# A fourth output weight split later, a fourth tile's sum begun earlier, and a last quarter taken by feature block, in the output projection of a decoder's second layer

## The chip, the core and the metric

The kernel runs on one core of a Trainium2 chip. The core has a matrix engine (TensorE, PE in the profile, with PEld for its weight loads), a vector engine (VectorE, DVE), a scalar engine (ScalarE, ACT), a general engine (GpSimd, POOL) and a queue engine (SyncE, SP), which here only starts transfers from the chip's memory. Each engine runs its own instructions in order; across engines they wait for each other by semaphores. The metric is the time of one execution on the device in microseconds, lower is better.

## What is computed

Two decoder layers on 512 tokens of 1024 features in float32. Layer A is a latent attention, layer B a sliding-window attention with 16 query heads of 64 features on 4 shared key and value heads. After each attention stands an output projection, a residual sum with layer norm, and a squared-ReLU MLP with its own norm. The change touches layer B's attention and output projection:

```python
def _swa(x, w_q, sinks, w_o, k_band, v_band, rel_bias):
    q = (x @ w_q).reshape(B, nb, BLOCK, SWA_KV_HEADS, G, SWA_HEAD_DIM)
    s = jnp.einsum('bnqkgd,bnjkd->bnkgqj', q, k_band).astype(jnp.float32) * SWA_HEAD_DIM ** -0.5
    ...
    p = (p / denom[..., None]).astype(x.dtype)
    o = jnp.einsum('bnkgqj,bnjkd->bnqkgd', p, v_band).reshape(B, S, SWA_Q_HEADS * SWA_HEAD_DIM)
    return o @ w_o

        ...
        x = _layernorm(alpha * x + y, ln_mix_g[l], ln_mix_b[l])
        x = _layernorm(alpha * x + _mlp(x, mlp_w_up[l], mlp_w_down[l]), ln_mlp_g[l], ln_mlp_b[l])
```

## The kernel before

**Splits.** Every float32 operand of a large product is split into a high and a low half (`split`, lines 75 to 84): ScalarE rounds the value into the high half (line 77), then VectorE, or GpSimd for some, subtracts that from the value for the low half (line 81). A product takes three matmuls per block of 128 features: high by high, high by low, low by high (`three`). Weights go through a stream (`queue`, `weights`, `prepare`): a weight tile of 128 by 1024 is loaded by SyncE into one of two `raw` buffers, and split into one of four pairs `wh` and `wl`. A raw buffer is free for the next load when the split has read it, a pair when the last matmul has read it. `fetchers` start a load ahead of its split, and `state["hold"]` says how far the stream may be prepared.

**Layer B's attention** is a hand-written software pipeline (`run_steps`): at step u it issues head u+2's scores and softmax, then some filling work, then head u's transposes (`turn`), and at each odd step the output of a pair of heads (`mix`). `mix` for heads 2m and 2m+1 leaves feature block m of the attention's output: TensorE multiplies probabilities and values, ScalarE copies half of each of two results (`low`, one buffer), VectorE adds (`o`), then ScalarE and GpSimd split `o` into `oh` and `ol`. Blocks 0 to 3 lie in the first tile of `oh` and `ol`, blocks 4 to 7 in the second. GpSimd also scales each head's probabilities (`p`, line 1449) and masks its transposed ones (`pm`, line 1469).

**The output projection** (`TokMajor`, object `proj`) has four token tiles t and two halves of the output's columns. Weight kp of a half covers feature blocks 2kp and 2kp+1. In the first half each token tile has a sum in PSUM, to which `part(t, kp)` adds six matmuls; after kp = 3 the sum is added to the residual on VectorE (line 638) and counted for the norm (line 631). The filling list places parts amid the attention:

```python
            for t, kp, u in ((0, 0, 11), (0, 1, 12), (1, 0, 12), (1, 1, 13), (2, 0, 14), (2, 1, 14), (0, 2, 15), (1, 2, 16), (2, 2, 16)):
                if (t, kp) == (1, 1):
                    fill.append((0, 13, 13, last_loads))
```

What the list leaves over, tile 3 and all of kp = 3, is done by `finish` after the last `mix`, weight by weight and tile by tile. Then `finish` takes the second half of the columns: four more weights, 24 matmuls for each token tile, each tile followed by its norm. `last_loads` prepares the fourth weight (load and split), fetches the seventh and eighth into a spare buffer, and lets the stream run on. The fourth weight's split is issued behind a softmax exponential (`"exp" if c == 3`).

The order of TensorE and of some transfers is the program's; the order on the other engines is made by a scheduler when the program is built, under the data's dependencies and the `behind` rules. While the second half runs, ScalarE and VectorE also split the MLP's first weights, into tiles `w_fac` and `w_quada`, whose room is the attention's.

Of the kernel before, what the change touches and what calls it, by code (L numbers as in the profile page):

```python
# [48 lines left out]
def build(tc, nc, io, out):  # L49
    with ExitStack() as top:  # L50
# [24 lines left out]
        def split(dst_h, dst_l, src, engine=None, keep=False):  # L75

            high = nc.scalar.activation(dst_h, src, AF.Copy)  # L77
            if keep:
                pe(high)
            with behind(state.pop("open", None)):  # L80
                low = (engine or nc.vector).tensor_sub(dst_l, src, f32(dst_h))  # L81
            if pinned[0] and engine is None:
                pe(low)
            return high, low
# [18 lines left out]
        def group(dst, pairs, first=True, last=True, **kw):  # L103
            for i, (st, mv) in enumerate(pairs):
                pe(nc.tensor.matmul(  # L105
                    dst, st, mv, start=first and i == 0, stop=last and i == len(pairs) - 1, **kw
                ))
# [207 lines left out]
            queue("w_sq", io["w_sq"][m], nc.gpsimd if m > 1 else nc.vector)  # L315
        first_so = len(stream)
        for c in range(8):
            queue("w_so", io["w_so"][c], nc.gpsimd if c in POOL_SO else nc.vector, "exp" if c == 3 else None)
        mlp_stream(1)

        ready = {}
# [199 lines left out]
        class TokMajor:  # L521
# [5 lines left out]
                self.src, self.evac, self.name = src, evac, name  # L527
                self.w, self.b, self.done = [], {}, set()

            def group(self, b, t, kp, w, cols=slice(0, 512)):  # L530
                tk = slice(t * P, (t + 1) * P)
                wh, wl = w
                for kk in range(2):
                    k, c = 2 * kp + kk, slice(kk * 512 + cols.start, kk * 512 + cols.stop)
                    group(b, three(self.src.h(k, tk), self.src.l(k, tk), wh[:, c], wl[:, c]), k == 0, k == 7)

            def part(self, t, kp):
# [4 lines left out]
                self.group(self.b[t], t, kp, self.w[kp])  # L542
                self.done.add((t, kp))
                if kp == 3:
                    self.evac(t, slice(0, 512), self.b[t])

            def finish(self, gb=None, dst=None, early=None, gb_at=None):

                for kp in range(4):
                    for t in range(NT):
                        if (t, kp) not in self.done:
                            self.part(t, kp)
                    if kp == gb_at:
                        gb = gb()
                if gb is not None:
                    ws = [weights(self.name) for _ in range(4)]
                    if callable(gb):
                        gb = gb()  # L560
                    for t in range(NT):
                        end = dst is None and t == NT - 1
                        n = 2 if end else 1
                        if end:
                            parts = last_tokens(gb)
                        for i in range(n):
                            c = slice(i * 512 // n, (i + 1) * 512 // n)
                            b = bank(512 // n)
                            for kp in range(4):
                                self.group(b, t, kp, ws[kp], c)  # L570
                            pinned[0] = early
                            with tc.high_priority():
                                self.evac(t, slice(512 + c.start, 512 + c.stop), b)
                            pinned[0] = False
                        pinned[0] = early
                        with tc.high_priority():
                            if end:
                                last_norm(gb, *parts)
                            else:
                                layer_norm(t, gb, dst)  # L580
                        if early:
                            prepare(early[t])
                        pinned[0] = False
                        if dst is not None and t in (1, 2):
                            with tc.high_priority():
# [730 lines left out]
        with tc.tile_pool(name="swa", bufs=1) as mp:  # L1316
# [120 lines left out]
            def weigh(h, bs, nb, sm, ri):  # L1437
                p = mp.tile([P, NT, P], F32, tag="p", bufs=3, name=nm("p"))
                for n in range(NT):
                    state["exp"] = nc.scalar.activation(  # L1440
                        p[:, n, :], bs[n // 2][:, n % 2, P:], AF.Exp, bias=nb[:, n : n + 1],
                        scale=SWA_SCALE, accum_out=sm[:, n : n + 1],
                    )
# [3 lines left out]
                nc.vector.reciprocal(ri, sm)  # L1447
                with tc.high_priority():
                    muls[h] = nc.gpsimd.tensor_mul(p, p, ri.unsqueeze(2).broadcast_to([P, NT, P]))
                ps_of[h] = p  # L1450
# [20 lines left out]
            def mix(h):  # L1471
# [7 lines left out]
                for n2 in range(2):  # L1479
# [18 lines left out]
                    for a, to in enumerate((lo, hi)):  # L1498
# [1 line left out]
                            o[to, n2, :].rearrange("p (n q) -> p n q", n=2),  # L1500
                            parts[lo, :, a, :], low[:, :, a, :],
                        )
                split(oh[m // 4][:, m % 4, :], ol[m // 4][:, m % 4, :], o.rearrange("p a b -> p (a b)"), nc.gpsimd)

            proj = TokMajor(Pair(oh, ol), add_scaled_last, "w_so")

            def last_loads():
                prepare(1)
                fetch_two(first_so + 6, xp.tile([P, 2, 1024], F32, tag="xt", bufs=8, name=nm("raw2")))
                state["hold"] = len(stream)  # L1510

            fill = []
# [136 lines left out]
```

## Time and profile before

| | |
|---|---|
| median of 3 runs | 993.61 us (993.2 to 993.73) |
| profiled execution | 994.75 us, its span 993.0 us |
| mean granted TensorE clock | 0.996 |
| TensorE busy, 493 to 620 us (layer B's keys to its attention's end) | 123.48 of 127.00 us |
| TensorE busy, 620 to 690 us (the output projection's rest and the MLP's start) | 68.56 of 70.00 us, clock 0.95 |

The span runs from the first to the last instruction of one profiled execution. Busy times of TensorE overlap with the next instruction's, since matmuls are pipelined: a matmul of 128 by 512 shows 0.39 us but starts 0.23 us after the one ahead. The granted clock is the share of full speed at which TensorE ran; that is why a row below 1 matters even where the engine shows no idle time. Names in the rows are the program's tiles without buffer numbers, and an idle time ahead of an instruction stands in brackets with the instruction that ended it.

### The profile page before, as it was taken

Reading aid. Unit: us, or ns where it says so; the run is one execution under the profiler, and the core shown is the slowest. Engines: PE = TensorE matmul, PEld = TensorE weight load, DVE = VectorE, ACT = ScalarE, POOL = GpSimd, SP = SyncE. Lnnn points to the kernel's source line nnn. Section 1 sums busy time; section 2 is a strip of 40 time slices with the busy share of each in tenths; the row PEclk is TensorE's granted clock in tenths of the full one; section 3 lists DMA queues with packets and bytes.
Section 4 is the critical chain, followed back from the end, with each engine's and each line's share of the span. In section 5 each row is a group of like instructions: output and inputs, shape, how many; then the busy total and the mean of one; then the engine's idle time right before and its main releaser. Section 6 shows DMA issues by size and latency. Waiting matters only on the chain.

```text
span 993.0 us, 15665 instructions
## 1 busy us (share of the span) xinstructions
PE 982.1 (99%) x6028; PEld 883.6 (89%) x6028; DVE 772.3 (78%) x1279; ACT 545.0 (55%) x842; POOL 239.0 (24%) x207
## 2 busy tenths in 40 slices
PE   9999999999999999999999998999999999999998
PEld 9888888998899999998898886889998999999986
DVE  6589858989768779786686787698885986898756
ACT  5557644467547537646146786436763663664620
POOL 1231101121312212210002997512131122022000
PEclk9999999999999999999999999899999999999999
DMA  7421236399888978964132223338896796898332
GB/s 262 145 88 43 93 120 201 54 230 220 146 198 227 168 169 224 224 106 147 65 107 96 86 92 132 106 65 147 268 183 121 233 214 116 223 261 147 84 127 85
DMA packets 60678, 149.54 MB, mean 151 GB/s; under 512 B 5259, under 2 KB 10300, under 8 KB 60604
## 3 DMA queue, kind: packets, MB, share of 16 engines
q0 software_dynamic: 24320, 58.73, 33.6%
q1 hardware_dynamic: 36140, 89.56, 26.2%
q8 instruction: 47, 0.77, 0.3%
q10 hardware_dynamic: 144, 0.26, 0.1%
q14 instruction: 27, 0.22, 0.1%
HBM read 146.41 MB, written 4.22 MB: 152 GB/s over the span
## 4 chain that ended last, share of the span: by engine, by line
PE 94%; DVE 2%; ACT 1%; POOL 1%; issue 0%; DMA 0%; DVEq 0%; POOLq 0%; ACTq 0%
PE mm L105 86%; PE tr L105 5%; PE tr L1243 1%; POOL wl L81 1%; PE tr L742 1%; ACT p L1440 1%; ACT wh L77 0%; PE tr L1465 0%; DMA raw<-in_w_h 0%; PE tr L507 0%; DVE o L1499 0%; POOL ol L81 0%; DVE pt L81 0%; DVE mm L1430 0%; PE tr L1007 0%
## 5 line engine op out<-in xcount | busy, mean ns | idle before, releaser
L105 PE MATMUL mm<-wh,fac 128*128 128x512 f32 (+1 forms) x944 | 292.7, 387 | 0.0
L77 ACT ACTIVATE wh<-wq 128x1024 fp32r<-128x1024 f32 x164 | 173.7, 1060 | 184.7 <-PE mm L105 138.4
L81 DVE TENSOR_TENSOR wl<-wq,wh 128x1024 fp32r<-128x1024 f32 x164 | 199.4, 1221 | 67.4 <-ACT wh L77 66.5
L105 PE MATMUL mm<-xth,wh 128*128 128x256 f32 (+1 forms) x928 | 243.8, 291 | 0.0
L105 PE MATMUL mm<-xth,wl 128*128 128x256 f32 (+1 forms) x800 | 233.8, 292 | 0.0
L105 PEld LDWEIGHTS mm<-wh,fac 128*128 128x128 f32 x944 | 176.4, 188 | 35.2 <-DVE fac L81 0.6
L105 PE MATMUL mm<-xtl,wh 128*128 128x256 f32 (+1 forms) x672 | 197.4, 294 | 0.0
L105 PE MATMUL mm<-wl,fac 128*128 128x512 f32 (+1 forms) x472 | 182.6, 387 | 0.0
L105 PEld LDWEIGHTS mm<-xth,wh 128*128 128x128 f32 x928 | 168.9, 192 | 3.0
L105 PEld LDWEIGHTS mm<-xth,wl 128*128 128x128 f32 x800 | 153.5, 192 | 2.7
L105 PEld LDWEIGHTS mm<-xtl,wh 128*128 128x128 f32 x672 | 128.9, 192 | 3.0
L77 ACT ACTIVATE wh<-raw 128x1024 fp32r<-128x1024 f32 (+3 forms) x86 | 85.0, 989 | 78.4 <-PE mm L105 53.2
L204 POOL DMA_DIRECT2D wq<-in_up x64 | 77.6, 1238 | 200.3 <-DVE wl L81 193.0
L105 PEld LDWEIGHTS mm<-wl,fac 128*128 128x128 f32 x472 | 88.9, 188 | 16.7
L81 DVE TENSOR_TENSOR wl<-raw,wh 128x1024 fp32r<-128x1024 f32 (+2 forms) x64 | 76.0, 1197 | 32.6 <-ACT wh L77 32.4
L204 POOL DMA_DIRECT2D wq<-in_down x48 | 42.0, 875 | 189.1 <-DVE wl L81 183.2
L81 POOL TENSOR_TENSOR wl<-raw,wh 128x1024 fp32r<-128x1024 f32 (+2 forms) x22 | 47.0, 2140 | 90.7 <-ACT wh L77 67.9
L105 PE MATMUL mm<-wh,oh 128*128 128x512 f32 x128 | 51.3, 400 | 3.2 <-ACT oh L77 3.2
L105 PE MATMUL mm<-wh,ol 128*128 128x512 f32 x128 | 50.8, 397 | 1.5 <-POOL ol L81 1.5
L105 PE MATMUL mm<-wl,oh 128*128 128x512 f32 x128 | 50.4, 394 | 0.1
L443 POOL TENSOR_TENSOR rs<-mv,half 128x1 f32<-128x1 f32 x16 | 8.8, 553 | 168.1 <-DVE mv L488 163.4
L641 DVE TENSOR_TENSOR x<-mm,x 128x512 f32<-128x512 f32 (+1 forms) x49 | 32.9, 675 | 15.6 <-PE mm L105 15.5
(246 smaller groups left out, 1791.1 us busy)
## 6 DMA issues: line engine op xcount, KB each, us to landing
wq<-in_up POOLq DMA_DIRECT2D x64, 512.0 KB, 7.3
wq<-in_down POOLq DMA_DIRECT2D x48, 512.0 KB, 7.1
wq<-in_up SPq DMA_DIRECT2D x32, 512.0 KB, 6.6
raw<-in_down SPq DMA_DIRECT2D x28, 512.0 KB, 6.1
wq<-in_down SPq DMA_DIRECT2D x24, 512.0 KB, 5.4
raw<-in_up SPq DMA_DIRECT2D x16, 512.0 KB, 4.7
raw<-in_w_o SPq DMA_DIRECT2D x8, 512.0 KB, 3.3
raw<-in_w_sq SPq DMA_DIRECT2D x8, 512.0 KB, 3.2
```

The costliest lines, as they stand in the source:

```text
L77: high = nc.scalar.activation(dst_h, src, AF.Copy)
L81: low = (engine or nc.vector).tensor_sub(dst_l, src, f32(dst_h))
L105: pe(nc.tensor.matmul(dst, st, mv, start=first and i == 0, stop=last and i == len(pairs) - 1, **kw))
L204: state["added", key, a, more, jp] = nc.gpsimd.dma_start(half(a, jp), chunk(*more, jp), accum_op=ALU.add)
L443: state["rs"] = nc.gpsimd.tensor_tensor(r, v, half, ALU.pow)
L641: nc.vector.tensor_add(xs[t][:, c], b, xs[t][:, c])
L742: pe(nc.tensor.transpose(pt[:, a, :], xs[t][:, k * P : (k + 1) * P], ident))
L1243: pe(nc.tensor.transpose(pt[:, kb * P : (kb + 1) * P], p[:, kb * P : (kb + 1) * P], ident))
L1440: state["exp"] = nc.scalar.activation(p[:, n, :], bs[n // 2][:, n % 2, P:], AF.Exp, bias=nb[:, n : n + 1], scale=SWA_SCALE, accum_out=sm[: ...
```

## The change

Four edits go together.

1. The fourth output weight is no longer prepared at step 13. `last_loads` only starts its load, and those of the seventh, eighth and fifth weights; a new `last_splits` at step 16 prepares it, and its split is issued behind the newest high split of an attention output (`state["oh"]`, there that of heads 12 and 13) and not behind an exponential.
2. Tile 3's first part joins the filling list, at step 15, ahead of tile 0's part with weight 2.
3. `part` and `group` take a list of feature blocks `kks`, and in layer B `finish` (`late=True`) takes the last weight by feature block: block 6 for all four tiles, then block 7 for all four.
4. `weigh` no longer keeps its exponential.

```diff
-            queue("w_so", io["w_so"][c], nc.gpsimd if c in POOL_SO else nc.vector, "exp" if c == 3 else None)
+            queue("w_so", io["w_so"][c], nc.gpsimd if c in POOL_SO else nc.vector, "oh" if c == 3 else None)
...
-            def group(self, b, t, kp, w, cols=slice(0, 512)):
+            def group(self, b, t, kp, w, cols=slice(0, 512), kks=range(2)):
...
-                for kk in range(2):
+                for kk in kks:
...
-                if kp == 3:
+                if kp == 3 and 1 in kks:
                     self.evac(t, slice(0, 512), self.b[t])
...
                 for kp in range(4):
+                    if late and kp == 3:
+                        for kk in range(2):
+                            for t in range(NT):
+                                self.part(t, kp, (kk,))
+                        continue
...
-                split(oh[m // 4][:, m % 4, :], ol[m // 4][:, m % 4, :], o.rearrange("p a b -> p (a b)"), nc.gpsimd)
+                state["oh"] = split(
+                    oh[m // 4][:, m % 4, :], ol[m // 4][:, m % 4, :], o.rearrange("p a b -> p (a b)"), nc.gpsimd
+                )[0]
...
             def last_loads():
+                fetchers[first_so + 3](raw_tile())
+                fetch_two(first_so + 6, xp.tile([P, 2, 1024], F32, tag="xt", bufs=8, name=nm("raw2")))
+                fetchers[first_so + 4](raw_tile())
+
+            def last_splits():
                 prepare(1)
-                fetch_two(first_so + 6, xp.tile([P, 2, 1024], F32, tag="xt", bufs=8, name=nm("raw2")))
                 state["hold"] = len(stream)
...
-            for t, kp, u in ((0, 0, 11), (0, 1, 12), (1, 0, 12), (1, 1, 13), (2, 0, 14), (2, 1, 14), (0, 2, 15), (1, 2, 16), (2, 2, 16)):
+            for t, kp, u in ((0, 0, 11), (0, 1, 12), (1, 0, 12), (1, 1, 13), (2, 0, 14), (2, 1, 14), (3, 0, 15), (0, 2, 15), (1, 2, 16), (2, 2, 16)):
                 if (t, kp) == (1, 1):
                     fill.append((0, 13, 13, last_loads))
+                if (t, kp) == (1, 2):
+                    fill.append((0, 16, 16, last_splits))
...
-            proj.finish(gb, x3, (0, 2, 0, 2))
+            proj.finish(gb, x3, (0, 2, 0, 2), late=True)
```

How instructions move is seen in the built programs' order. First TensorE at head 14's transposes (`tr` from `p`). The sums of tiles 0, 2 and 3 are mm_6398, mm_6567 (mm_6565 in the changed program) and, in the changed one, mm_6588; wh_6256 is weight 2, wh_5976 weight 0; oh_5171 and oh_5172 are the two tiles of `oh`. Before:

```order
L105 MATMUL mm_6567<-wh_6116,ol_5173 128x512
L1465 MATMUL tr_6582<-ident,p_6458 128x128 x4
L105 MATMUL mm_6398<-wh_6256,oh_5172 128x512
L105 MATMUL mm_6398<-wl_6257,oh_5172 128x512
L105 MATMUL mm_6398<-wh_6256,ol_5174 128x512
```

In the changed program:

```order
L105 MATMUL mm_6565<-wh_6116,ol_5173 128x512
L1470 MATMUL tr_6580<-ident,p_6458 128x128 x4
L105 MATMUL mm_6588<-wh_5976,oh_5171 128x512
L105 MATMUL mm_6588<-wl_5977,oh_5171 128x512
L105 MATMUL mm_6588<-wh_5976,ol_5173 128x512
```

Six matmuls of tile 3 (the three rows stand twice) have come between the transposes and tile 0's part with weight 2.

Second, ScalarE from head 15's exponentials on. wh_6520 is the fourth weight before, wh_6634 the fourth and wh_6691 the fifth in the changed program; `oh_5172<-o_6542` (o_6540) is heads 10 and 11's output, `o_6616` (o_6609) that of 12 and 13. Before:

```order
L77 ACTIVATE wh_6520<-raw_6519 128x1024
L1497 ACTIVATE low_6548<-tr_6543 64x512
L1445 ACTIVATE mm_6493<-nb_6490,sink 128x4
L77 ACTIVATE pt_6580<-tr_6582 128x4x128
L1497 ACTIVATE low_6561<-mm_6552 64x512
L77 ACTIVATE oh_5172<-o_6542 128x512
L77 ACTIVATE pt_6580<-tr_6608 128x4x128
L1497 ACTIVATE low_6622<-tr_6617 64x512
L1497 ACTIVATE low_6635<-mm_6626 64x512
L77 ACTIVATE oh_5172<-o_6616 128x512
```

In the changed program:

```order
L1502 ACTIVATE low_6546<-tr_6541 64x512
L1450 ACTIVATE mm_6493<-nb_6490,sink 128x4
L1502 ACTIVATE low_6559<-mm_6550 64x512
L77 ACTIVATE pt_6578<-tr_6580 128x4x128
L77 ACTIVATE oh_5172<-o_6540 128x512
L77 ACTIVATE pt_6578<-tr_6601 128x4x128
L1502 ACTIVATE low_6615<-tr_6610 64x512
L1502 ACTIVATE low_6628<-mm_6619 64x512
L77 ACTIVATE oh_5172<-o_6609 128x512
L77 ACTIVATE wh_6634<-raw_6519 128x1024
L77 ACTIVATE wh_6691<-raw_6524 128x1024
```

The fourth weight's split has gone from ahead of heads 10 and 11's output to behind that of heads 12 and 13, and the fifth weight's has come up behind it. On GpSimd the low half of heads 10 and 11's output has passed one masking (`pm`) forward.

Third, VectorE from the last output on. The x rows add the four tiles' first halves to the residual; wl_6598 before, and wl_6697 in the changed program, is the sixth weight's low half; w_fac and w_quada are the MLP's first weights. Before:

```order
L1499 TENSOR_TENSOR o_6653<-mm_6663,low_6672 64x256 x2
L81 TENSOR_TENSOR wl_6592<-raw_6590,wh_6591 128x1024
L81 TENSOR_TENSOR wl_6598<-raw_6596,wh_6597 128x1024
L638 SCALAR_TENSOR_TENSOR x_1598<-x_1598,mm_6398 128x512
L631 BN_STATS bn_6712<-x_1598 128x6
L81 TENSOR_TENSOR w_fac_6750<-wq_6395,w_fac_6750 128x1024
L638 SCALAR_TENSOR_TENSOR x_1600<-x_1600,mm_6473 128x512
L635 TENSOR_SCALAR bn_6712<-bn_6712 128x1
L81 TENSOR_TENSOR w_quada_6753<-wq_6395,w_quada_6753 128x1024
```

In the changed program:

```order
L1504 TENSOR_TENSOR o_6650<-mm_6660,low_6669 64x256 x2
L643 SCALAR_TENSOR_TENSOR x_1598<-x_1598,mm_6398 128x512
L81 TENSOR_TENSOR w_fac_6750<-wq_6395,w_fac_6750 128x1024
L643 SCALAR_TENSOR_TENSOR x_1600<-x_1600,mm_6473 128x512
L636 BN_STATS bn_6721<-x_1598 128x6
L643 SCALAR_TENSOR_TENSOR x_1602<-x_1602,mm_6565 128x512
L81 TENSOR_TENSOR w_quada_6753<-wq_6395,w_quada_6753 128x1024
L643 SCALAR_TENSOR_TENSOR x_1604<-x_1604,mm_6588 128x512
L636 BN_STATS bn_6728<-x_1600 128x6
L640 TENSOR_SCALAR bn_6721<-bn_6721 128x1
L81 TENSOR_TENSOR wl_6697<-raw_6695,wh_6696 128x1024
```

The sixth weight's low half has moved from ahead of the residual sums to behind all four of them and both MLP weights. The fifth weight's (wl_6592 before) has gone forward, ahead of the last output. ScalarE splits the sixth weight behind `w_fac` and `w_quada` too.

More of the change, by code (lines that the diff above doesn't have):

```diff
@@ L528, in __init__, with part @@
                 self.w, self.b, self.done = [], {}, set()
-            def group(self, b, t, kp, w, cols=slice(0, 512)):
+            def group(self, b, t, kp, w, cols=slice(0, 512), kks=range(2)):
                 tk = slice(t * P, (t + 1) * P)
                 wh, wl = w
-                for kk in range(2):
+                for kk in kks:
                     k, c = 2 * kp + kk, slice(kk * 512 + cols.start, kk * 512 + cols.stop)
                     group(b, three(self.src.h(k, tk), self.src.l(k, tk), wh[:, c], wl[:, c]), k == 0, k == 7)
-            def part(self, t, kp):
+            def part(self, t, kp, kks=range(2)):
                 while len(self.w) <= kp:
@@ L541, in part, with finish @@
                     self.b[t] = bank()
-                self.group(self.b[t], t, kp, self.w[kp])
+                self.group(self.b[t], t, kp, self.w[kp], kks=kks)
                 self.done.add((t, kp))
-                if kp == 3:
+                if kp == 3 and 1 in kks:
                     self.evac(t, slice(0, 512), self.b[t])
-            def finish(self, gb=None, dst=None, early=None, gb_at=None):
+            def finish(self, gb=None, dst=None, early=None, gb_at=None, late=False):
                 for kp in range(4):
+                    if late and kp == 3:
[3 more added lines that the diff above has]
+                        continue
                     for t in range(NT):
@@ L1439, in weigh @@
                 for n in range(NT):
-                    state["exp"] = nc.scalar.activation(
+                    nc.scalar.activation(
                         p[:, n, :], bs[n // 2][:, n % 2, P:], AF.Exp, bias=nb[:, n : n + 1],
```

## The prediction

> **What bounds the kernel now.** The page comes first: the busy table and the chain that ended last.
>
> ```profile
> PE 982.1 (99%) x6028; PEld 883.6 (89%) x6028; DVE 772.3 (78%) x1279; ACT 545.0 (55%) x842; POOL 239.0 (24%) x207
> PE 94%; DVE 2%; ACT 1%; POOL 1%; issue 0%; DMA 0%; DVEq 0%; POOLq 0%; ACTq 0%
> ```
>
> TensorE sets the end almost everywhere. The change can win only where TensorE waits or runs slowly. The waits between 600 and 654 us show one such place:
>
> ```profile
> PE mm L105 <- ACT oh L77: 3.2, 1, 3.2
> PE mm L105 <- POOL ol L81: 1.5, 1, 1.5
> ```
>
> The timeline of TensorE shows where (start, duration, instruction; idle time before it in brackets), and the windows show the granted clock (after the five engines' busy times, the column before the DMA share):
>
> ```profile
> 614.66 0.60 PE L1465 MATMUL tr<-ident,p 128*128 128x128 f32 x4
> 615.01 0.48 PE L105 MATMUL mm<-wh,oh 128*128 128x512 f32 x1
> 615.57 0.39 PE L105 MATMUL mm<-wh,ol 128*128 128x512 f32 x1
> 619.13 0.50 PE L105 MATMUL mm<-wh,oh 128*128 128x512 f32 x1 [3.18 <-ACT oh L77]
> ...
> 621.34 0.80 PE L105 MATMUL mm<-wh,ol 128*128 128x512 f32 x1 [1.47 <-POOL ol L81]
> ...
> 627.45 0.40 PE L105 MATMUL mm<-wl,oh 128*128 128x512 f32 x1
> ...
> 629.28 0.62 PE L105 MATMUL tr<-pt,vv 128*128 128x512 f32 x2
> ...
> 630.92 0.40 PE L105 MATMUL mm<-wh,oh 128*128 128x512 f32 x1
> ...
> 640.47 0.39 PE L105 MATMUL mm<-wh,oh 128*128 128x512 f32 x1
> ```
>
> ```profile
> 619.10:621.90 2.80, 1.29 (x3) 0.71 (x4) 0.00 (x0) 0.00 (x0) 2.18 (x2) 0.77 0.00 0
> 621.90:625.80 3.90, 3.90 (x18) 3.67 (x17) 1.42 (x3) 1.19 (x2) 1.38 (x1) 0.50 0.02 4
> ```
>
> Token tile 0 reaches weight pair 2 at 615.01. Its first feature block runs; the second needs the output of heads 10 and 11, whose high half comes at 619.1 and low half at 621.3. The clock then falls to half and is back at 627.45. The 42 matmuls from 630.92 to 640.47 give the full pace, 0.2275 us each; four transposes take 0.35 (614.66 to 615.01), one head pair's output 1.64 (629.28 to 630.92). Between 615.80 (615.57 and one pace) and 627.45 stand three matmuls, four transposes, one output and four matmuls, 3.60 us at full pace. They took 11.65. **The stall costs 8.05 us**, of which 2.85 is the half clock after 621.34 (6.11 elapsed for 3.26 of work).
>
> Why the output is late:
>
> ```profile
> 611.98 1.07 ACT L77 ACTIVATE wh<-raw 128x1024 fp32r<-128x1024 f32 x1
> 612.92 1.85 POOL L1469 TENSOR_TENSOR pm<-pt,tri 128x768 fp32r<-128x768 f32 x1
> 613.09 2.77 DVE L81 TENSOR_TENSOR wl<-raw,wh 128x1024 fp32r<-128x1024 f32 x1 [1.75 <-ACT wh L77]
> ...
> 615.36 0.60 ACT L77 ACTIVATE pt<-tr 128x512 fp32r<-128x512 f32 x1 [1.53 <-PE tr L1465]
> 615.77 0.84 DVE L1499 TENSOR_TENSOR o<-tr,low 64x256 f32<-64x256 f32 x2
> ...
> 617.26 1.04 POOL L1449 TENSOR_TENSOR p<-p,ri 128x512 f32<-128x512 f32 x1 [2.49 <-DVE ri L1447]
> 618.25 1.81 POOL L1469 TENSOR_TENSOR pm<-pt,tri 128x768 fp32r<-128x768 f32 x1
> 618.45 0.63 ACT L77 ACTIVATE oh<-o 128x512 fp32r<-128x512 f32 x1 [1.15 <-DVE o L1499]
> ...
> 620.02 1.26 POOL L81 TENSOR_TENSOR ol<-o,oh 128x512 fp32r<-128x512 f32 x1
> ```
>
> The fourth weight's split stands ahead of the output on ScalarE (611.98) and VectorE, where it lasts 2.77 us because GpSimd is reading until 614.77. The split of the output, 620.02, then stands behind two more GpSimd operations.
>
> **The change, part by part.** The split leaves that place, and six matmuls of tile 3 come ahead of the waiting tile 0. ScalarE is free at 611.98; copy, sum, copy, sum (0.60, 0.84, 0.60, 0.84) end near 615.0. The high split follows the copy of 615.36 on ScalarE and ends near 616.5. GpSimd has done the probabilities by 615.8 (614.77 and 1.04), and now takes the low split before the masking, to 617.8. Tile 0's second block is reached at 615.80 plus six paces, 617.17, and asks for the low half at 617.63. A wait of 0.25 stays. **The 8.05 us go.**
>
> From there TensorE runs at pace: transposes from 618.1, output of heads 12 and 13 to 620.1, twelve matmuls, last output to 624.45, tile 3's twelve, twelve on block 6, and block 7 begins at 629.9, its first low half asked for at 630.4. The chain that brings it: output of heads 12 and 13 summed by 622.6, its high split to 623.25, low split to 624.65. Behind it on ScalarE come the two moved weight splits, to 625.2; on VectorE the fourth weight's low half waits for GpSimd until 624.65, and the next weight's ends at 626.8. Only then comes the last output's sum, copy, sum, to 629.2, its high split to 629.9 and its low split to **E = 631.2**. TensorE waits 0.85, and reaches the second half at 633.5. So far 8.05 less 1.1 is won.
>
> Reordering the last quarter by feature block changes no instruction count. Its 24 matmuls are the same 24; what it buys is 2.7 us of cover for heads 14 and 15, used above.
>
> **What is late next.** The sixth weight (second half, pair 1) loads into the ring slot that the fourth one's split frees at 625.7, where before it was freed at 615.86:
>
> ```profile
> 615.88 0.33 SPq L142 DMA_DIRECT2D raw<-in_w_so  x1
> ...
> 614.66:619.10 4.44, 1.29 (x8) 0.82 (x6) 3.60 (x8) 1.82 (x3) 1.95 (x3) 1.00 0.37 118
> ```
>
> 118 GB/s over 4.44 us is that one load of 512 KB, so it lands within 3.2 us: near 629 now, in time. Behind it on SP stand the norm's two loads, which wait for the last output's low half as before, and the MLP's loads. One of those now waits until the sixth weight's split frees its ring slot, and holds those behind it; they feed products that come after the second half's 96 matmuls, 21.8 us at the pace, so I charge nothing. Without that cover they would cost what they are late. But its split has moved behind the MLP weights on ScalarE, and on VectorE behind three evacuations, those two splits, a fourth evacuation and two statistics. Durations:
>
> ```profile
> 636.20 1.05 ACT L77 ACTIVATE w_fac<-wq 128x1024 fp32r<-128x1024 f32 x1
> 637.15 1.04 ACT L77 ACTIVATE w_quada<-wq 128x1024 fp32r<-128x1024 f32 x1
> ...
> 637.45 2.39 POOL L81 TENSOR_TENSOR wl<-raw,wh 128x1024 fp32r<-128x1024 f32 x1
> ...
> 638.30 2.62 DVE L81 TENSOR_TENSOR w_fac<-wq,w_fac 128x1024 fp32r<-128x1024 f32 x1
> ...
> 641.51 1.21 DVE L81 TENSOR_TENSOR w_quada<-wq,w_quada 128x1024 fp32r<-128x1024 f32 x1
> 641.81 3.18 POOL L81 TENSOR_TENSOR wl<-raw,wh 128x1024 fp32r<-128x1024 f32 x1 [1.98 <-ACT wh L77]
> ...
> 642.64 0.68 DVE L638 SCALAR_TENSOR_TENSOR x<-x,mm 128x512 f32<-128x512 f32 x1
> 643.24 0.68 DVE L631 BATCH_NORM_STATS2 bn<-x 128x6 f32<-128x512 f32 x1
> ```
>
> A weight's low half on VectorE takes 1.13 from start to start (641.51 to 642.64), an evacuation or statistic 0.60 (642.64 to 643.24), a big ScalarE split 0.95. These rows also show the two engines shutting each other out: w_fac took 2.62, ending 1.08 after GpSimd's split at 639.84; GpSimd's 641.81 took 3.18, ending 2.27 after VectorE's at 642.72. Who is served when one waits and the other queues more:
>
> ```profile
> 550.72 2.41 POOL L81 TENSOR_TENSOR wl<-raw,wh 128x1024 fp32r<-128x1024 f32 x1
> ...
> 552.37 1.04 DVE L81 TENSOR_TENSOR vv<-vf,vv 128x256 fp32r<-128x256 f32 x1
> ...
> 553.09 2.03 POOL L1469 TENSOR_TENSOR pm<-pt,tri 128x768 fp32r<-128x768 f32 x1
> ```
>
> VectorE waited out 550.72's instruction and went next: the masking that followed took 2.03 and not 1.85.
>
> The first MLP weight's ScalarE split waits for E in the changed program. VectorE after E: evacuation at 0.60 (TensorE resumes at E+0.06; a matmul after a wait lasts 0.50), w_fac 1.20, evacuation 2.33, statistic 2.93, evacuation 3.53, w_quada 4.13. ScalarE finishes weight seven at E+3.97 (0.06, three times 0.95, 1.06), so GpSimd starts its low half at E+4.04. Two ends follow. GpSimd first: it runs to 6.4, w_quada to 7.55, evacuation, statistics to 8.85, but GpSimd is in weight eight until 9.85, so the sixth weight is ready at E+10.95. VectorE first: GpSimd's split runs from 5.3 to 7.65, and the sixth weight is ready at E+8.75. Without any shutting out, it would still be E+7.85. TensorE asks at 635.1, E+3.9. **I take GpSimd first**, by the 0.09 us, a narrow choice: a new stall of 7.05 us; the other end is 4.85.
>
> Both idle stretches are as long as the old one (4.65 of the 5.5 us before 621.34), so the half clock follows: 2.85 by the rows above. Bounds: nothing if the clock stays; at most 3.35, since 0.77 over 2.8 us puts its fall near 620.6, and 6.7 us of half pace to 627.3 cost that if all lay behind the resumption.
>
> The Trainium skill, page "TensorE: Matmul & The Clock Gate", Part 1, says that the clock halves after an idle window of about 3.4 us and returns after a busy one, the windows running freely. By that the spell after a resumption lasts 3.4 to 6.8 us and costs 1.7 to 3.4, an estimate from that page; the forecast would be 995.2 to 996.9.
>
> One old wait disappears, since weight eight is ready before TensorE gets there:
>
> ```profile
> 644.55 0.39 PE L105 MATMUL mm<-wh,oh 128*128 128x512 f32 x1
> 645.04 0.50 PE L105 MATMUL mm<-wl,oh 128*128 128x512 f32 x1
> ```
>
> 0.49 less a pace, 0.26. Sum: -8.05 + 1.1 + 7.05 + 2.85 - 0.26 = +2.7 us. The profiled execution took 994.75 for a span of 993.0, the runs' median is 993.61; a difference carries over, so **996.3**.
>
> **Rivals.** (1) VectorE gets the shared way first: 4.85 in place of 7.05, **994.1**. For it: 0.09 us is finer than these rows can promise. Against: the order worked out. (2) VectorE first, and the clock stays up: **991.25**, faster. It decides if 4.85 us of idleness in one piece does not do what two pieces did. Against: the old idleness was no longer. By the skill's clock page, free windows could split 4.85 into parts that are each short of 3.4; the same time follows. (3) The sixth weight is not late at all: -8.05 + 1.1 - 0.26, **986.4**. It takes a VectorE that needs under 3.9 us for what its rows add up to 7.85. (4) The change doesn't remove the first wait, because heads 10 and 11's output is late for another reason, or E itself comes later: each us of E is one us; with the old low half's time, 3.7 us at 617.63, about **999.8**. Against: the sums at 615.77 began just as VectorE's 2.77 us ended.
>
> **How the numbers follow.** Chances: forecast 0.48, (1) 0.30, (2) 0.10, (3) 0.05, (4) 0.07. A measurement tells 0.2%, 2 us, from no change: 991.6 and 995.6. The forecast falls below 995.6 only with a short clock spell (0.05 of its 0.48); (1) lies within, but for 0.03 below. Faster 0.10 + 0.05 + 0.03 = 0.18, same 0.27 + 0.05 = 0.32, slower 0.43 + 0.07 = 0.50. The forecast's own range is 995 to 997.4 (half clock between 1.5 and 3.35, E by half a us). The range for eight in ten takes in (1) and (2), with E half a us early: 990.8 to 997.6; (3), most of (4) and the edges are left out.
>
> **What would show it.** Right: no wait of TensorE on oh near 617; waits under 1 us for ol at 617.6 and 630.4; the half clock gone from 621 to 627 and found again behind a wait of 5 to 7 us on VectorE's wl, ahead of the second half's eighth matmul, near 635; VectorE showing w_quada stretched past 3 us. Wrong: second-half matmuls running through at 0.2275 from 633.5, or that wait below 4 us, or full clock after it.

## The result, and the profile after

The changed kernel takes 996.51 us (median of 8 runs, 995.91 to 997.64), the kernel before 993.67 (8 runs on the same chip): a ratio of 1.0029, 95% interval 1.0018 to 1.0040. The change makes the kernel slower by 0.3%. The forecast was 996.3.

The profiled execution took 995.91 us for a span of 994.1, with a mean clock of 0.997. Busy table and chain:

```profile
PE 980.7 (99%) x6028; PEld 881.9 (89%) x6028; DVE 771.6 (78%) x1279; ACT 544.5 (55%) x842; POOL 239.0 (24%) x207
PE 94%; DVE 2%; ACT 1%; issue 1%; POOL 1%; DVEq 0%; ACTq 0%; POOLq 0%
```

They say nothing of what happened: the instruction counts are those of before, and the shares nearly so. The waits of TensorE between 600 and 660 us do:

```profile
PE mm L105 <- DVE wl L81: 6.6, 1, 6.6
PE mm L105 <- POOL ol L81: 0.6, 1, 0.6
```

The 3.2 us on `oh` and the 1.5 on `ol` are gone; one wait of 6.6 us on a weight's low half has come. TensorE's timeline and the granted clock show both places:

```profile
613.80 0.60 PE L1470 MATMUL tr<-ident,p 128*128 128x128 f32 x4
...
617.02 0.50 PE L105 MATMUL mm<-wh,ol 128*128 128x512 f32 x1
...
630.58 0.50 PE L105 MATMUL mm<-wh,ol 128*128 128x512 f32 x1 [0.62 <-POOL ol L81]
...
634.35 0.39 PE L105 MATMUL mm<-wh,oh 128*128 128x512 f32 x1
...
641.32 0.80 PE L105 MATMUL mm<-wl,oh 128*128 128x512 f32 x1 [6.58 <-DVE wl L81]
...
646.12 0.39 PE L105 MATMUL mm<-wh,oh 128*128 128x512 f32 x1
```

```profile
638.50:639.00 0.50, 0.00 (x0) 0.00 (x0) 0.50 (x2) 0.28 (x1) 0.50 (x1) 1.00 0.00 0
639.00:640.00 1.00, 0.00 (x0) 0.00 (x0) 1.00 (x3) 0.00 (x0) 1.00 (x1) 0.60 0.00 0
...
645.50:646.00 0.50, 0.50 (x3) 0.41 (x2) 0.00 (x0) 0.46 (x1) 0.00 (x0) 0.50 1.05 393
```

This execution runs 0.86 us ahead of before's already at head 14's transposes (613.80 against 614.66), which stand ahead of TensorE's first moved instruction; the same row stands between 613.7 and 614.7 in the other kernels below, so intervals are compared here, not absolute times. The second half's eighth matmul, due one pace after 634.35, starts at 641.32: 6.74 us late. The eleven matmuls from it on take 4.80 us, at full pace 2.50: the half clock costs 2.30. This execution is the fastest of the eight; four of the others, 996.51 to 997.64, show a mean clock of 0.993 in place of 0.997, and no trace of those was kept.

Why the sixth weight is late, from GpSimd's rows and VectorE's:

```profile
629.25 1.28 POOL L81 TENSOR_TENSOR ol<-o,oh 128x512 fp32r<-128x512 f32 x1 [5.31 <-ACT oh L77]
634.54 5.64 POOL L81 TENSOR_TENSOR wl<-raw,wh 128x1024 fp32r<-128x1024 f32 x2 [3.37 <-ACT wh L77]
```

```profile
631.72 1.22 DVE L81 TENSOR_TENSOR w_fac<-wq,w_fac 128x1024 fp32r<-128x1024 f32 x1
...
634.64 3.34 DVE L81 TENSOR_TENSOR w_quada<-wq,w_quada 128x1024 fp32r<-128x1024 f32 x1
...
639.15 2.12 DVE L81 TENSOR_TENSOR wl<-raw,wh 128x1024 fp32r<-128x1024 f32 x1
```

The last output's low half ends at 630.53 (the prediction's E). GpSimd begins the seventh weight at 634.54, VectorE w_quada at 634.64, and w_quada lasts 3.34 us in place of about 1.2. Then VectorE makes the sixth weight; it is done at 641.27, 1.09 us after GpSimd's two splits end at 640.18 and 10.74 after E.

### The profile page after: what moved, and what is told of

It is laid out like the page before. It is cut to its first block, busy times and chain, and to the rows that moved or that the text cites. A ratio compares the mean times of both kernels' runs of the same rounds, so it can differ in the third digit from the quotient of the medians.

```text
span 994.1 us, 15663 instructions
## 1 busy us (share of the span) xinstructions
PE 980.7 (99%) x6028; PEld 881.9 (89%) x6028; DVE 771.6 (78%) x1279; ACT 544.5 (55%) x842; POOL 239.0 (24%) x207
## 4 chain that ended last, share of the span: by engine, by line
PE 94%; DVE 2%; ACT 1%; issue 1%; POOL 1%; DVEq 0%; ACTq 0%; POOLq 0%
PE mm L105 87%; PE tr L105 5%; PE tr L1248 1%; PE tr L747 1%; POOL ol L81 1%; ACT p L1445 0%; PE tr L1470 0%; DVE o L1504 0%; PE tr L507 0%; DVE w_quada L81 0%; POOL wl L81 0%; DVE pt L81 0%; PE tr L1012 0%; DVE mm L1435 0%; DVE wl L81 0%
## 5 line engine op out<-in xcount | busy, mean ns | idle before, releaser
L105 PEld LDWEIGHTS mm<-wl,fac 128*128 128x128 f32 x472 | 88.8, 188 | 16.5
```

The source lines that it names most:

```text
L105: pe(nc.tensor.matmul(dst, st, mv, start=first and i == 0, stop=last and i == len(pairs) - 1, **kw))
```

## The experiments

**The theory** is the prediction's: the old stall is won, and a late sixth weight and a half clock give it back. **The rivals**: the sixth weight only shows slack, and another limit stands right behind it; GpSimd takes nothing from VectorE; the half clock is free; other parts of the change carry the gain or the loss. Each kernel had 5 to 11 runs; its ratio is to the kernel before, on the same chip.

| kernel | us | ratio, 95% interval |
|---|---|---|
| changed | 996.51 | 1.0018 to 1.0040 |
| changed, sixth weight early | 989.50 | 0.9947 to 0.9972 |
| changed, sixth weight early and split early | 988.24 | 0.9932 to 0.9957 |
| changed, no weight split on GpSimd there | 993.66 | 0.9982 to 1.0001 |
| changed, TensorE kept busy in the stall | 993.96 | 0.9996 to 1.0014 |
| before, TensorE kept busy in the old stall | 991.67 | 0.9971 to 0.9990 |
| before and the early quarter alone | 994.21 | 0.9999 to 1.0017 |
| late split alone | 991.96 | 0.9975 to 0.9992 |
| late split and early quarter | 992.72 | 0.9980 to 0.9998 |
| late split and block order | 996.11 | 1.0015 to 1.0033 |
| sixth weight early and split early, no block order | 991.06 | 0.9964 to 0.9982 |
| sixth weight early and split early, no early quarter | 988.63 | 0.9933 to 0.9961 |
| sixth weight early and split early, seventh on VectorE | 988.54 | 0.9931 to 0.9957 |

### The sixth weight loaded early

```diff
                 fetch_two(first_so + 6, xp.tile([P, 2, 1024], F32, tag="xt", bufs=8, name=nm("raw2")))
                 fetchers[first_so + 4](raw_tile())
+                fetchers[first_so + 5](xp.tile([P, 2, 1024], F32, tag="xt", bufs=8, name=nm("raw3"))[:, 0, :])
```

> One line added to the changed kernel: the sixth output weight is loaded into a free buffer of its own, beside the seventh and eighth, and no longer waits for the ring slot that the fourth weight's split frees; its split therefore comes between the last output's two sums instead of behind the MLP weights and the evacuations. Nothing computed changes. Theory (the stall of 6.7 us on the sixth weight's low half, and the half clock of some 2.3 us behind it, give the won 8 us back): the stall near 641 goes, the last output's low half comes about 1.3 us later because VectorE does the weight between its two sums, and TensorE waits about 1.8 us there in place of 0.8: 996.5 - 6.7 - 2.3 + 1.0 = about 988.5. Rival (the sixth weight is only where slack shows; another limit stands right behind it, the seventh or eighth weight or the evacuations): the wait moves to the next weight and the time stays at 994 to 997.

989.50 us: 7.0 below the changed kernel, 8.0 expected. TensorE's timeline:

```profile
630.51 0.50 PE L105 MATMUL mm<-wh,oh 128*128 128x512 f32 x1 [0.46 <-ACT oh L77]
...
632.27 0.50 PE L105 MATMUL mm<-wh,ol 128*128 128x512 f32 x1 [1.03 <-POOL ol L81]
...
646.54 1.09 PE L747 MATMUL tr<-ident,x 128*128 128x128 f32 x8 [0.81 <-DVE x L495]
```

VectorE now makes the sixth weight's low half at 627.53, between the last output's two sums. No wait on a weight is left and the clock stays at 1, so no other limit of that size stood right behind. The waits for the last output have grown to 0.46 and 1.03, as expected; the missing 1 us is for the most part a new wait of 0.8 on the norm.

### The sixth weight loaded early and split behind the output

```diff
-            queue("w_so", io["w_so"][c], nc.gpsimd if c in POOL_SO else nc.vector, "oh" if c == 3 else None)
+            queue("w_so", io["w_so"][c], nc.gpsimd if c in POOL_SO else nc.vector, "oh" if c in (3, 5, 6) else None)
```

on top of the early load.

> As the run before it, and the sixth and seventh weights' splits are put behind the newest output's high split, as the change does with the fourth: so VectorE makes the last output's two sums first, then the sixth weight, then the evacuations. Nothing computed changes. Theory: both the stall on the sixth weight and the late last output go; only the two waits under 1 us for low halves stay: 996.5 - 6.7 - 2.3 = about 987.5, and up to 1 us less than the kernel with the early load alone. Rival (another limit right behind): 994 to 997.

988.24 us, the fastest of all: 5.4 below before and 8.3 below the changed kernel (987.5 expected). The timeline keeps the wait for the last output, and one of 0.35 for GpSimd's first weight:

```profile
631.00 0.50 PE L105 MATMUL mm<-wh,ol 128*128 128x512 f32 x1 [0.64 <-POOL ol L81]
...
638.22 0.50 PE L105 MATMUL mm<-wl,oh 128*128 128x512 f32 x1 [0.35 <-POOL wl L81]
```

Two variants of it change nothing that can be told from it.

> The fastest kernel so far without the early quarter of the fourth token tile. Nothing computed changes. Theory (six matmuls moved between two waits): 0.55 us more, 988.8. Rival (the early quarter costs time): 987.5.

Without the early quarter: 988.63 us (988.17 to 988.96, against 987.75 to 988.40).

> The fastest kernel so far with the seventh weight's low half on VectorE in place of GpSimd. Nothing computed changes. Theory (the wait of 0.35 us on GpSimd's low half near 638 is what is left there, and VectorE has 1.1 us to spare once GpSimd no longer stretches w_fac): 987.9, 0.3 us less. Rival (the evacuations behind that split come later and the norm waits for them): 988.5 to 989.5.

With the seventh weight on VectorE (`POOL_SO` without 6): 988.54 us (987.85 to 988.73). The wait on the weight goes, and one of 0.5 us for the norm's sum comes, as the rival said.

### No weight split on GpSimd near the second half

```diff
-POOL_O, POOL_SO = (0, 2), (0, 1, 2, 6, 7)
+POOL_O, POOL_SO = (0, 2), (0, 1, 2)
```

> The changed kernel with the low halves of the seventh and eighth weights made by VectorE, so GpSimd has nothing to do near the second half's start, and the sixth weight keeps its place in VectorE's queue. Nothing computed changes. Theory (of the new stall, about 2.9 us come from VectorE and GpSimd shutting each other out, the rest from the sixth weight's place behind two MLP weights and the evacuations): sixth weight ready 7.85 us after the last output's low half in place of 10.74, the stall 3.8 in place of 6.7; with the half clock as before 993.6, and 991.3 if the clock stays up after the shorter stall. Rival (it is the place in the queue alone; GpSimd's work costs VectorE nothing on balance, since the seventh and eighth weight now stand on VectorE): 996 to 998.

993.66 us; 993.6 was expected. The rows of GpSimd, VectorE and TensorE, and the clock:

```profile
629.93 1.27 POOL L81 TENSOR_TENSOR ol<-o,oh 128x512 fp32r<-128x512 f32 x1 [5.31 <-ACT oh L77]
```

```profile
635.33 1.22 DVE L81 TENSOR_TENSOR w_quada<-wq,w_quada 128x1024 fp32r<-128x1024 f32 x1
...
637.72 1.22 DVE L81 TENSOR_TENSOR wl<-raw,wh 128x1024 fp32r<-128x1024 f32 x1
```

```profile
638.99 0.50 PE L105 MATMUL mm<-wl,oh 128*128 128x512 f32 x1 [3.58 <-DVE wl L81]
...
640.72 0.80 PE L105 MATMUL mm<-wl,oh 128*128 128x512 f32 x1
```

```profile
640.25:640.50 0.25, 0.25 (x2) 0.00 (x0) 0.25 (x1) 0.00 (x0) 0.00 (x0) 1.00 0.22 74
640.50:640.75 0.25, 0.18 (x2) 0.04 (x1) 0.25 (x2) 0.00 (x0) 0.00 (x0) 0.53 1.19 385
...
644.00:644.25 0.25, 0.25 (x3) 0.20 (x2) 0.00 (x0) 0.13 (x1) 0.00 (x0) 1.00 1.03 401
```

w_quada and the weight take 1.22 each, not 3.34 and 2.12. The sixth weight is ready at 638.94, 7.74 us after E (631.20 here), 3.0 us sooner, and the wait is 3.58. What GpSimd's two splits cost VectorE is thereby measured. The clock still falls, but at about 640.5, after TensorE has been running at full clock for 1.5 us. And not always: of the 11 runs seven took 993.3 to 994.3 at a mean clock of 0.995 to 0.997, four 990.9 to 991.1 at 0.999. The groups' medians lie 2.8 us apart. The half clock in this trace (993.27 us, mean clock 0.997) lasts 3.4 us and so accounts for at most 1.7; five of the seven show 0.995, which would be longer spells, but no trace of one was kept. The second group lies near the 991.25 that rival (2) gave for a stall without half clock.

### TensorE kept busy in the stall

Zeros are multiplied into a bank that nobody reads, in the changed kernel (26 matmuls ahead of the second half's second pair) and in the kernel before (13 ahead of tile 0's second block on pair 2). The first of the two edits:

```diff
+                                if self.name == "w_so" and (t, kp) == (0, 1):
+                                    group(
+                                        tbank().rearrange("p (a b) -> p a b", a=4),
+                                        [(zeros, zeros[:, None, :].broadcast_to([P, 4, P]))] * 26,
+                                    )
                                 self.group(b, t, kp, ws[kp], c)
```

> The changed kernel with 26 extra matmuls of zeros into a bank that nobody reads, ahead of the second half's matmuls that wait for the sixth weight; at 0.2275 us each they fill 5.9 us of the 6.7 us stall. They add work and change no output. Theory (the stall ends by VectorE, and TensorE then pays some 2.3 us of half clock because it had been idle): the stalled matmul starts at the same time, the granted clock stays near 1 behind it, and the time is 996.5 - 2.3 = about 994.2. Rival (the half clock costs nothing, since the evacuations or the seventh and eighth weight set the pace of those 4 us anyway): 996.5. If the zeros delay the stalled matmul instead, 997 or more.

993.96 us: 2.55 less, with all the work that was there and more. The timeline:

```profile
634.81 6.10 PE L105 MATMUL tr<-zeros 128*128 128x512 f32 x26
...
641.92 0.50 PE L105 MATMUL mm<-wl,oh 128*128 128x512 f32 x1 [0.78 <-DVE wl L81]
```

Counted from head 14's transposes the waiting matmul starts at 27.65 us (641.92 less 614.27), in the changed kernel at 27.52, so the stall ends where it did, and the clock behind it is 1. The half clock thus goes with the idle time, and the typical run pays about 2.5 us for it.

> The kernel before with 13 extra matmuls of zeros into a bank that nobody reads, ahead of tile 0's second feature block on pair 2; at 0.2275 us each they fill 2.96 us of the 3.2 us for which TensorE waits there for heads 10 and 11's high half. They add work and change no output. Theory (the old stall's 8.05 us are 5.2 us of waiting and 2.85 of half clock behind it): the two waits end at the same times, the clock stays at 1 behind them, and the time is 993.7 - 2.85 = 990.8. Rival (the half clock there costs nothing, since the last output is waited for later anyway): 993.7, with a wait of some 3 us for the last output near 632.

991.67 us, 1.74 less than the kernel before on that chip (993.41); 2.85 was expected. The wait for the low half ends where it ended (621.40, before 621.34). The zeros themselves start only at 616.77 and push the high half's matmul from 619.13 to 619.84; that costs nothing, because the low half comes later:

```profile
621.40 0.50 PE L105 MATMUL mm<-wh,ol 128*128 128x512 f32 x1 [0.94 <-POOL ol L81]
...
626.58 0.62 PE L105 MATMUL tr<-pt,vv 128*128 128x512 f32 x2
```

The profiled executions do differ by 2.70 (this output started at 629.28 before), and their spans by 2.7 (990.3 and 993.0). But the profiled run of before, 994.75, lay 1.1 us above its median of 993.67. By the medians the half clock costs the typical run less than that one; the interval of the ratio, 0.9971 to 0.9990, is 1.0 to 2.9 us, so 2.85 stands at its very edge.

### One part alone, and one part less

First the early quarter alone, in the kernel before: `(3, 0, 15)` added to the list.

> The kernel before with the early quarter of the fourth token tile alone: its six matmuls on weight pair 0 come ahead of tile 0's pair 2; the fourth weight's split stays where it was. Nothing computed changes. Theory (the late output of heads 10 and 11 sets that stall, and the six matmuls only lie inside it): the two waits near 619 and 621 end at the same times, the half clock follows as before, and what is won is at most the six matmuls, 1.37 us: 992.2 to 993.6. Rival (the early quarter is what removes the stall): some 8 us less, about 986, unless a new wait follows.

994.21 us, not to be told from before; the theory's upper end was 993.6. The waits in this kernel:

```profile
PE mm L105 <- POOL ol L81: 3.3, 2, 2.3
PE mm L105 <- ACT oh L77: 1.8, 1, 1.8
```

The wait for the high half shrinks from 3.2 to 1.8, by the six matmuls, and all of it returns: 2.3 for the low half, where before had 1.5, and 1.0 for the last output's. The low half doesn't end at the same time, as the theory had it, but 7.68 us after head 14's transposes (621.72 less 614.04) and not 6.68. Its split shows why:

```profile
619.42 2.25 POOL L81 TENSOR_TENSOR ol<-o,oh 128x512 fp32r<-128x512 f32 x1
```

It took 1.26 us before. The six matmuls are the last that read weight pair 0, so the fifth weight's split came forward, and VectorE makes its low half from 617.84 to 620.54, while GpSimd is at the output's. Moving six matmuls moved a weight's split too.

The changed kernel without the early quarter and with the last quarter by token tile (`finish` without `late=True`) is the late split alone:

> The changed kernel without the early quarter of the fourth token tile and without the order by feature block: what is left is the fourth weight's split behind the output of heads 12 and 13, with the loads. Nothing computed changes. Theory (the split's place is what removed the old stall; what follows is set by VectorE's and GpSimd's queues behind the last output): no wait on the high half near 617, a wait of about 1.6 us for heads 10 and 11's low half in place of 0.25, 2 to 3 us for the last output's, and a wait of 2 us or more on the sixth weight, since its place in VectorE's queue stays: 993 to 995.5. Rival (the other two edits carry the gain): the wait on oh near 617 stays and the time is that of before or more.

991.96 us, below the expected 993 to 995.5. TensorE's rows:

```profile
616.51 0.50 PE L105 MATMUL mm<-wh,oh 128*128 128x512 f32 x1 [0.56 <-ACT oh L77]
...
617.86 0.50 PE L105 MATMUL mm<-wh,ol 128*128 128x512 f32 x1 [0.62 <-POOL ol L81]
...
630.06 0.50 PE L105 MATMUL mm<-wh,oh 128*128 128x512 f32 x1 [0.43 <-ACT oh L77]
...
631.41 0.50 PE L105 MATMUL mm<-wh,ol 128*128 128x512 f32 x1 [0.62 <-POOL ol L81]
...
639.47 0.50 PE L105 MATMUL mm<-wl,oh 128*128 128x512 f32 x1 [1.88 <-DVE wl L81]
```

The old stall is down to 0.56 and 0.62 us, so the split's place is what removed it; a short wait on the high half stays, which the theory had not. The last output is waited for 1.05 us and not 2 to 3, since E is no later than in the changed kernel (16.71 us after head 14's transposes, there 16.73). The wait on the sixth weight is there. These rows are of the slowest of the 11 runs (993.47 us), with a half clock from 639.85 to 643.25. In 7 runs, 991.4 to 992.1 us, the mean clock was 1.0: the half clock mostly doesn't come.

The last quarter by token tile, with the early quarter kept:

> The changed kernel with the last quarter by token tile again, as before the change; the early quarter of tile 3 and the late split stay. Nothing computed changes. The order by feature block put the first half's evacuations close together behind the last output; by token tile they are spread, and VectorE's order is evacuation, w_fac, statistic, evacuation, w_quada, so that w_quada may begin ahead of GpSimd's split in place of 0.1 us behind it. Theory (VectorE's and GpSimd's queue behind the last output sets the end): the wait for the last low half grows by 2.05 us to 2.85, but the sixth weight is ready 8.2 us after that low half in place of 10.7 and is asked for 2.05 us later, a wait of about 2.2 in place of 6.7: 991.8 if the clock stays up, 994 if it halves. Rival (the order by feature block is worth its 2 us of cover): 998.5.

992.72 us, between the two ends; the order by feature block costs 3.8 us in the changed kernel where it should buy 2. VectorE's, GpSimd's and TensorE's rows:

```profile
634.05 1.22 DVE L81 TENSOR_TENSOR w_quada<-wq,w_quada 128x1024 fp32r<-128x1024 f32 x1
...
636.45 2.15 DVE L81 TENSOR_TENSOR wl<-raw,wh 128x1024 fp32r<-128x1024 f32 x1
```

```profile
629.26 1.27 POOL L81 TENSOR_TENSOR ol<-o,oh 128x512 fp32r<-128x512 f32 x1 [5.30 <-ACT oh L77]
634.56 6.30 POOL L81 TENSOR_TENSOR wl<-raw,wh 128x1024 fp32r<-128x1024 f32 x2 [3.38 <-ACT wh L77]
```

```profile
638.66 0.50 PE L105 MATMUL mm<-wl,oh 128*128 128x512 f32 x1 [1.87 <-DVE wl L81]
```

Here w_quada begins 0.51 us ahead of GpSimd's split and lasts 1.22. The sixth weight comes ahead of the fourth evacuation and is ready 8.07 us after E (8.2 expected; 10.74 in the changed kernel), and TensorE asks for it later. The half clock behind it lasts 3.4 us in place of 6.8.

> The fastest kernel so far (sixth weight loaded early, its and the seventh weight's split behind the newest output's) with the last quarter by token tile. Nothing computed changes. Theory (where VectorE's queue is out of the way, the order by feature block does what it is for): the wait for the last low half grows from 0.8 to about 2.85 us, nothing else changes: 988.2 + 2.05 = 990.3. Rival (the order is worth nothing, because the 2 us are taken back before the second half's weights are ready): 988.2.

991.06 us; 990.3 was expected. So the order by feature block is worth 2.8 us where the sixth weight is not late: the 2.05 of cover, and a rest of 0.8 that goes with a half clock from 631.2 to 634.6, which the longer idle time brings (that the two are cause and effect was not tried).

The order by feature block without the early quarter:

> The changed kernel without the early quarter of the fourth token tile; the late split and the order by feature block stay. Nothing computed changes. Theory (the early quarter only moves six matmuls, 1.37 us, between two waits): the wait for heads 10 and 11 grows by some 1.3 us, the wait of 0.8 for the last low half goes, since TensorE comes there 1.3 us later than in the changed kernel while that output is no later; the second half begins about 0.55 us later and the stall on the sixth weight and the half clock are as in the changed kernel: 997.1. Rival (the last output comes as much later as TensorE does): 997.9. Rival (the early quarter costs time, as a comparison of the kernel with the split alone, 991.96, to the one by token tile, 992.72, might suggest): 995.7.

996.11 us, 1.0 below what the theory said and 0.4 above the second rival, but not to be told from the changed kernel: the intervals overlap. The rows show the slip:

```profile
629.37 1.29 POOL L81 TENSOR_TENSOR ol<-o,oh 128x512 fp32r<-128x512 f32 x1 [5.32 <-ACT oh L77]
634.68 5.64 POOL L81 TENSOR_TENSOR wl<-raw,wh 128x1024 fp32r<-128x1024 f32 x2 [3.38 <-ACT wh L77]
```

TensorE does come later, but GpSimd's splits start and last as in the changed kernel (20.75 us after head 14's transposes, there 20.74). They follow E and ScalarE's splits behind it, not TensorE, and the sixth weight follows them: the matmul that waits for it starts 27.54 us after head 14's transposes, there 27.52. The early quarter was put in or left out in four kernels (before, late split, changed, fastest), and in each pair the two intervals overlap: it is worth nothing that can be told.

## Why the prediction was right

**The old stall goes** (-8.05). Right: no wait on `oh`, 0.24 and 0.79 us for the low halves, where 0.25 and 0.85 stood, and the late split alone does it. Its share of half clock, 2.85, was right for the profiled execution (2.70 by the kernel with zeros), but by the medians the typical run pays 1.74. That is the step that was off in size: "a difference carries over" from one execution to the median need not hold for a clock term. The 3.26 us set for the work behind 621.34 don't follow from the prediction's own prices (five matmuls, four transposes and an output make 3.13; with zeros it took 3.37), which moves this term by 0.1 us.

**The new stall** (+7.05): 6.74, ready 10.74 us after E, not 10.95. The early load takes the stall away and its cost with it, so the theory stands. Its parts are measured: 3.0 us are GpSimd's, the rest is the place behind two MLP weights and the evacuations.

**GpSimd first, by 0.09 us**: by 0.10, and by 0.09 in the kernel with zeros (635.03 against 635.12), so it was not one execution's chance. With VectorE 0.51 us ahead (last quarter by token tile) w_quada isn't stretched, so the fine order did decide, but it was not the only thing that differed there. Rival (1) held as a mechanism and not as the case.

**The half clock behind it** (+2.85): 2.30 in the profiled execution, 2.55 by the kernel with zeros. Rival (2) is near the truth at a shorter stall: with 3.58 us of it, 4 of 11 runs lie at 991 us with a mean clock of 0.999.

**How long the half clock lasts.** The Trainium skill, page "TensorE: Matmul & The Clock Gate", Part 1, has the clock judged over free-running windows of about 3.4 us. The half-clock spells here are 6.8 us in the changed kernel (639.2 to 646) and 3.4 with no split on GpSimd (640.5 to 643.9), two and one such windows, and the estimate worked out from that page of the Trainium skill, 995.2 to 996.9, holds the result. The Trainium skill's page has the clock halve after an idle window; here it also fell after 3.4 us in which TensorE was busy for over 40% (last section), and the measurement decides.

**Rival (3)**, 986.4 if the sixth weight were not late, is what the repaired kernel comes near to with 988.24. **Rival (4)** did not hold: no wait on `oh` was left, and E came 16.73 us after head 14's transposes; 631.2 less 614.66 is 16.5.

**The sum.** With the measured terms, -8.05 + 1.03 + 6.74 + 2.30 - 0.26 = +1.8; from head 14's transposes to the end, the profiled executions differ by 1.96 (994.1 less 613.80, 993.0 less 614.66). With the half clocks of the typical run, 1.74 and 2.55, the same sum gives +3.1; the medians differ by 2.84. The forecast of +2.7 is near them because the misses, 1.1 us in the old half clock, 0.3 each the other way in the new one and in the stall, partly cancel. The mechanism was right; that the number came within 0.2 us was luck.

What was missed is the order by feature block. The prediction says that "what it buys is 2.7 us of cover". By token tile, tile 0's block 6 stands ahead of the wait as well, so the order buys nine matmuls, 2.05 us. It also brings the residual sums together behind the last output, which puts w_quada behind GpSimd's split. The sum has both, but never sets the cover against them: by token tile the changed kernel is 3.8 us faster.

## What to carry to other kernels

When a split or load is moved later, follow its ring slot: the next load into it moves too, and what was made early may come to stand last in another engine's queue. The same holds for a matmul that is the last to read a weight. Cover on TensorE is worth little if the reordering that buys it lets the next thing waited for come later. Check the transfer behind the moved one first: one line that gave the sixth weight a buffer of its own turned a loss of 2.8 us into a gain of 4.1.

## What was not expected

**Matmuls that run again do not always save the clock.** With no split on GpSimd, TensorE had been running for 1.5 us at full clock when it fell at 640.5. Of the 3.4 us before that fall it was busy for 44%; in the kernel with the late split and the early quarter, whose windows stand here, for 45%.

```profile
639.25:639.50 0.25, 0.25 (x3) 0.21 (x2) 0.25 (x1) 0.00 (x0) 0.25 (x1) 1.00 0.00 0
639.50:639.75 0.25, 0.25 (x2) 0.19 (x1) 0.25 (x2) 0.00 (x0) 0.25 (x1) 0.64 0.86 66
...
643.00:643.25 0.25, 0.25 (x2) 0.20 (x2) 0.00 (x0) 0.25 (x1) 0.00 (x0) 1.00 1.03 393
```

The matmul that had waited there started at 638.66, 0.9 us before the fall at 639.6, and the spell lasts 3.4 us. So a fall can come well after the end of the wait that it goes with. The busy share of some 3.4 us does not decide by itself: in the same kernel TensorE was busy for 41% of the time from 626.8 to 630.2, and the clock stayed at 1. How busy TensorE must be, and when, was not measured.

**Where the clock falls, the times spread.** Kernels in which the clock falls behind a stall, in all runs or some, spread over 1.3 us or more (before 992.6 to 995.2 in 21 runs, no split on GpSimd 990.9 to 994.3). The kernels in which it stays up spread over 0.65 to 1.0. Two of these had 11 runs, so it is not the number of runs: they are the two kernels with zeros, which spread over 0.8 and 1.0 where the same kernels without them spread over 1.7 and 1.8. A wide spread may be a first sign of such a stall.
